# The experts' weight loads move from SyncE's DMA queue to GpSimd's

## The chip, the cores and the metric

The kernel runs on one core of one Trainium2 chip. The core has TensorE (PE, the matmuls), VectorE (DVE), ScalarE (ACT), GpSimd (POOL) and SyncE (SP), and 16 DMA engines that move data between HBM and the on-chip memory SBUF. A transfer is issued by one engine's instruction stream, in the order of the program, and goes into a queue that belongs to the issuer: in this kernel SP's transfers are in the queue that the profile calls q1 hardware_dynamic, and GpSimd's are in q0 software_dynamic. The metric is the device time of one execution in microseconds (us), lower is better.

## The reference, cut to what matters

One layer over 1024 tokens of width 1024. A mixer (a state-space scan and a gated short convolution, projected in and out) comes first; it is unchanged here. Then a mixture of 32 experts follows: the router picks two experts for each token, every expert computes `(silu(x @ w_gate) * (x @ w_up)) @ w_down` on its tokens with a hidden width of 512, and the two results of a token are added with their gates. A root-mean-square norm ends the layer.

```python
h  = x + mixer(rmsnorm(x))
hn = rmsnorm(h)
ys = lax.map(run_block, (xs, block_expert))          # (silu(xb @ w_gate[e]) * (xb @ w_up[e])) @ w_down[e]
out = zeros.at[row_token].add(ys * row_gate[:, None])
return rmsnorm(h + out)
```

All weights are float32. One expert has three matrices of 2 MB, so that the 32 experts bring in 201 MB, each byte used once.

## The kernel before, in words

The program is one long, hand-ordered instruction stream. Its first part, up to about 800 us, is the mixer in two halves of 512 tokens. Its second part walks over the experts. Each expert has a place for up to 96 tokens (`CAP`); what doesn't fit is done by a loop at the end, which runs no iteration on these data.

**Weights.** Each of the 96 matrices (32 experts, gate, up and down) comes in two halves of 1 MB, [128 partitions x 2048 floats], which makes 192 halves numbered q. `order` (line 785) is the order of the matrices: gate and up of the next expert stand before down of the present one. A half lands in one of 15 places (`HALVES`, line 792), which are regions of SBUF that the mixer left free: SC, P1, Y, P2 and WR hold two each, TA four, N one. `load_m` (line 816) issues the load of half q, by SP. The first 15 loads (q 0 to 14) are put into the stream by hand, at the end of the mixer. From then on `reuse` (line 800) issues one load each time a half has been used up: the place becomes the home of the next half. `reuse` also retires places: N is never reused, and a place of TA, WR, P2 or P1 is given up when the loads are more than `lead` halves ahead. `lead` falls from 15 to 8, and is 4 from the 150th half on (`Q1`, `LEAD1`), where only the four places in SC and Y are left.

**Splits and matmuls.** A half is used as two chunks of [128 x 1024], 384 chunks c in all. `split_m(c)` writes each chunk as two float32r parts into one of four W buffers: the high part by ACT (line 80), the rest by DVE (line 86). After the second chunk of a half it calls `reuse`. In loop step c (line 1222) PE multiplies chunk c, then whatever `between` holds for this place is put into the stream, then chunk c + 4 is split. Each chunk feeds six matmuls of 512 columns (lines 1123 to 1125 for gate and up, 1134 to 1136 for down).

**Gathers and scatters.** These are the indirect transfers, and GpSimd issues them. `gather(e)` (line 1093) fetches the rows of expert e's tokens from `hg_d` into one of two buffers GX; it is issued two experts ahead, after `tok_trans(e - 2)` (line 1109) has read the buffer. `down_out(e)` scales the result by ACT (line 1156) into one of four buffers YE and adds it to the rows of `acc_d` by an indirect transfer with addition (line 1157). Each scatter waits for the scatter before it, since both add to `acc_d`. Slots without a token carry an index out of bounds and move nothing.

**The end.** `fin_load` (line 1191) waits for the last scatter of the loop, of expert 30, and then loads the sums by SP, 8 tiles of 512 KB (line 1195). `fin_norm` (line 1199) normalises and stores them, and `fin_last` adds expert 31's result.

Which part is ordered by what: SP's and GpSimd's instructions run in program order, each after its waits. The loads wait for DVE's split of the half that lay in the place before. In the program, the loads from q 15 on stand between the gathers and scatters: the load of q 15 stands before the first gather, and the loads from q 16 on after it.

Of the kernel before, what the change touches and what calls it, by code (L numbers as in the profile page):

```python
# [35 lines left out]
def layer(ctx: ExitStack, tc: tile.TileContext, x, norm_mix, w_in, ssd_conv_w, ssd_conv_b, dt_bias,  # L36
# [16 lines left out]
    def region(tag, shape, dt=F32):  # L53
        return rg.tile(shape, dt, name=tag, tag=tag)
# [22 lines left out]
    act, dve, pe, pool, sp = nc.scalar, nc.vector, nc.tensor, nc.gpsimd, nc.sync  # L77
# [716 lines left out]
    NR = len(HALVES)  # L794
# [5 lines left out]
    def reuse(q):  # L800


        n = len(place)
        lead = max(LEAD, NR - q // FALL) if q < Q1 else LEAD1
        if HALVES[place[q]][0] == "N" or n - q > lead and HALVES[place[q]][0] in TAGS:
            return
        place[n] = place[q]
        load_m(n)

    def raw_half(q):  # L810
        tag, i = HALVES[place[q]]
        if tag not in raw:
            raw[tag] = region(tag, [P, {"TA": 8192, "N": 2048}.get(tag, 4096)])
        return raw[tag][:, i * 2048:(i + 1) * 2048]

    def load_m(q):
        if q < 2 * len(order):
            kind, e = order[q // 2]
            src = {"g": w_gate, "u": w_up, "d": w_down}[kind]
            sp.dma_start(raw_half(q), src[e, q % 2])  # L820

    def split_hi(c):
        copy_a(W[(NB + c) % 4][:, 0], raw_half(c // 2)[:, c % 2 * 1024:(c % 2 + 1) * 1024])
# [12 lines left out]
    for h in range(2):  # L836
# [25 lines left out]
        if h == 1:  # L862
            for q, n in enumerate((44, 44, 45, 46, 51, 47, 49, 55, 56, 57, 57, 58, 58)):
                at(b0 + n, load_m, q)
# [95 lines left out]
    h_stats(1, KD - 2)  # L960
    h_stats(1, KD - 1)
    load_m(13)
    load_m(14)
    reuse(0)
# [257 lines left out]
    for c in range(end):  # L1222
        kind, e = order[c // 4]
# [61 lines left out]
```

## Time and profile before

| | |
|---|---|
| median of 3 runs | 1439.19 us (1437.18 to 1439.37) |
| the profiled execution, its own time | 1442.68 us |
| its span, first to last instruction | 1440.8 us |
| mean granted TensorE clock | 0.98 |
| busy: PE, weight loads of PE, DVE, ACT, POOL | 95%, 72%, 71%, 62%, 9% |
| q1 hardware_dynamic (SP) | 291.06 MB, 56.0% of 16 engines' span |
| q0 software_dynamic (GpSimd) | 30.44 MB, 8.5% |

A busy share is the time in which an engine executes instructions, over the span; DMA shares are means over the 16 DMA engines. A row such as "POOL L1157 <- ACT N" says that an instruction of line 1157 on POOL had to wait, and that the last thing it waited for was an ACT instruction that writes N. The profiled execution is 3.5 us over the median.

### The profile page before, as it was taken

The page shows a single profiled execution, that of the slowest core. Times are in us where ns is not written, and L with a number is a line of the kernel's source. Part 1 is how long each engine was busy: PE and PEld are TensorE (multiplying, and loading weights), DVE is VectorE, ACT ScalarE, POOL GpSimd, SP SyncE. Part 2 cuts the span into 40 slices and gives each one's busy share as a digit, 9 for nine tenths or more (in the row PEclk, how much of TensorE's full clock was granted, in tenths as well). Part 3 has the DMA queues.
Part 4 walks back from the last instruction along what each step waited for, and adds up shares of the span by engine and source line. Part 5 has one row for each costly group of instructions (what it writes and reads, how often), then busy time and mean ns, then how long its engine had stood idle before and what let it go on. Part 6 is the DMA issues. An engine that isn't in the chain of part 4 may idle for free. (4 is left out here: it accounts for less than half of the span.)

```text
span 1440.8 us, 17497 instructions
## 1 busy us (share of the span) xinstructions
PE 1362.1 (95%) x6459; PEld 1044.3 (72%) x6459; DVE 1029.4 (71%) x1356; ACT 890.9 (62%) x1343; POOL 132.2 (9%) x123
## 2 busy tenths in 40 slices
PE   6999999999999999999999499999999999999992
PEld 4888888878878878888788376677777777776661
DVE  5755676664467776765643589999989998988884
ACT  5655434365365544433643487788888888887783
POOL 0000100200000000000000101111111111112110
PEclk9999999999999999999999699999999999999995
DMA  6333332543444233225565779899999999999996
GB/s 192 133 99 106 116 93 88 135 165 118 125 145 133 95 111 117 73 88 147 212 212 183 257 287 347 308 367 352 361 363 368 363 360 371 375 352 318 348 331 242
DMA packets 128453, 322.64 MB, mean 224 GB/s; under 512 B 8960, under 2 KB 89012, under 8 KB 103789
## 3 DMA queue, kind: packets, MB, share of 16 engines
q1 hardware_dynamic: 117164, 291.06, 56.0%
q0 software_dynamic: 11200, 30.44, 8.5%
q8 instruction: 51, 0.84, 0.2%
q14 instruction: 38, 0.30, 0.1%
HBM read 304.71 MB, written 25.30 MB: 229 GB/s over the span
## 5 line engine op out<-in xcount | busy, mean ns | idle before, releaser
L86 DVE TENSOR_TENSOR W<-WR,W 128x1024 fp32r<-128x1024 f32 (+1 forms) x162 | 195.1, 1209 | 108.7 <-ACT W L80 108.5
L1124 PE MATMUL acc<-W,TB 128*96 128x512 f32 x512 | 202.6, 396 | 5.6 <-DVE W L86 5.6
L1123 PE MATMUL acc<-W,TB 128*96 128x512 f32 x512 | 204.5, 399 | 0.7 <-ACT W L80 0.7
L1125 PE MATMUL acc<-W,TB 128*96 128x512 f32 x512 | 203.1, 397 | 0.0
L80 ACT ACTIVATE W<-WR 128x1024 fp32r<-128x1024 f32 (+1 forms) x162 | 168.3, 1043 | 34.2 <-PE acc L274 18.3
L257 PE MATMUL acc<-TA,W 128*128 128x512 f32 x416 | 165.7, 398 | 1.9 <-ACT tk L529 1.9
L257 PE MATMUL acc<-TB,W 128*128 128x512 f32 x416 | 166.0, 399 | 1.2 <-ACT tk L529 1.2
L259 PE MATMUL acc<-TB,W 128*128 128x512 f32 x416 | 162.3, 390 | 0.0
L259 PE MATMUL acc<-TA,W 128*128 128x512 f32 x416 | 162.3, 390 | 0.0
L258 PE MATMUL acc<-TA,W 128*128 128x512 f32 x416 | 162.0, 389 | 0.0
L258 PE MATMUL acc<-TB,W 128*128 128x512 f32 x416 | 162.0, 389 | 0.0
L86 DVE TENSOR_TENSOR W<-SC,W 128x1024 fp32r<-128x1024 f32 x96 | 114.4, 1218 | 20.0 <-ACT W L80 19.0
L86 DVE TENSOR_TENSOR W<-Y,W 128x1024 fp32r<-128x1024 f32 x92 | 109.4, 1218 | 15.0 <-ACT W L80 14.9
L1124 PEld LDWEIGHTS acc<-W,TB 128*96 128x96 f32 x512 | 83.1, 162 | 42.6 <-DVE W L86 9.0
L1125 PEld LDWEIGHTS acc<-W,TB 128*96 128x96 f32 x512 | 82.8, 162 | 35.8 <-DVE TB L86 0.4
L1123 PEld LDWEIGHTS acc<-W,TB 128*96 128x96 f32 x512 | 83.0, 162 | 35.1 <-ACT W L80 1.6
L80 ACT ACTIVATE W<-SC 128x1024 fp32r<-128x1024 f32 x96 | 98.6, 1057 | 13.1 <-DMA SC<-in_w_up_dram 6.8
L1135 PE MATMUL sd<-W,TB 128*96 128x512 f32 x256 | 102.4, 400 | 3.8 <-DVE W L86 3.8
L86 DVE TENSOR_TENSOR W<-P,W 128x1024 fp32r<-128x1024 f32 x80 | 95.4, 1218 | 13.5 <-ACT W L80 13.2
L1134 PE MATMUL sd<-W,TB 128*96 128x512 f32 x256 | 104.1, 407 | 1.0 <-ACT TB L80 0.6
L80 ACT ACTIVATE W<-Y 128x1024 fp32r<-128x1024 f32 x92 | 94.9, 1058 | 15.3 <-DMA Y<-in_w_up_dram 5.9
L1136 PE MATMUL sd<-W,TB 128*96 128x512 f32 x256 | 102.1, 399 | 0.0
(306 smaller groups left out, 2444.2 us busy)
## 6 DMA issues: line engine op xcount, KB each, us to landing
WR<-in_w_in_dram SPq DMA_DIRECT2D x44, 1024.0 KB, 5.1
SC<-in_w_down_dram SPq DMA_DIRECT2D x18, 1024.0 KB, 11.0
WR<-in_w_out_dram SPq DMA_DIRECT2D x16, 1024.0 KB, 6.3
SC<-in_w_gate_dram SPq DMA_DIRECT2D x16, 1024.0 KB, 12.1
P<-in_w_up_dram SPq DMA_DIRECT2D x16, 1024.0 KB, 9.1
Y<-in_w_up_dram SPq DMA_DIRECT2D x16, 1024.0 KB, 13.1
Y<-in_w_gate_dram SPq DMA_DIRECT2D x15, 1024.0 KB, 14.2
TA<-in_w_down_dram SPq DMA_DIRECT2D x15, 1024.0 KB, 9.9
```

Of the source, the lines that this page charges most:

```text
L80: act.activation(o, i, AF.Copy, scale=scale)
L86: dve.tensor_tensor(o, a, b, op=op)
L257: pe.matmul(o, w[:, 0, k], t[:, 0, k], start=start and k == 0, stop=False)
L258: pe.matmul(o, w[:, 0, k], t[:, 1, k], start=False, stop=False)
L259: pe.matmul(o, w[:, 1, k], t[:, 0, k], start=False, stop=stop and k == KD - 1)
L1123: pe.matmul(pt, a[:, 0, k], w[:, 0, q], start=k == 0, stop=False)
L1124: pe.matmul(pt, a[:, 0, k], w[:, 1, q], start=False, stop=False)
L1125: pe.matmul(pt, a[:, 1, k], w[:, 0, q], start=False, stop=k == KD - 1)
L1134: pe.matmul(pt, a[:, 0, k], w[:, 0, n], start=k == 0, stop=False)
L1135: pe.matmul(pt, a[:, 0, k], w[:, 1, n], start=False, stop=False)
L1136: pe.matmul(pt, a[:, 1, k], w[:, 0, n], start=False, stop=k == 3)
```

## The change

`load_m` issues the halves q 0 to 15 by SP as before (`NR` is 15), and the halves from 16 on, 176 of the 192, by GpSimd. Nothing else is edited: each load stands at the same place of the program and has the same source, destination and size. It is now in GpSimd's instruction stream, between the gathers and scatters, and in their DMA queue.

```diff
         if q < 2 * len(order):
             kind, e = order[q // 2]
             src = {"g": w_gate, "u": w_up, "d": w_down}[kind]
-            sp.dma_start(raw_half(q), src[e, q % 2])
+
+            (sp if q <= NR else pool).dma_start(raw_half(q), src[e, q % 2])
```

## Rows read from the trace of the kernel before

**Rows 1.** Busy time of each engine in stretches of the experts' part: stretch, its length, busy us (and instructions) of PE, PE's weight loads, DVE, ACT and POOL, granted clock, DMA share, GB/s.

```profile
934.00:952.00 18.00, 18.00 (x87) 12.77 (x86) 16.29 (x17) 15.21 (x19) 3.24 (x2) 1.00 0.99 358
...
1262.00:1280.00 18.00, 18.00 (x88) 12.77 (x87) 16.30 (x17) 15.39 (x19) 3.59 (x3) 1.00 1.02 374
...
1317.00:1337.00 20.00, 18.75 (x87) 12.53 (x87) 16.03 (x16) 15.04 (x19) 3.92 (x3) 1.00 1.00 359
1337.00:1357.00 20.00, 18.09 (x84) 12.10 (x82) 16.08 (x16) 14.37 (x19) 3.52 (x2) 1.00 0.98 347
```

**Rows 2.** GpSimd's instructions in order of time, here scatters (line 1157): start, us, line, what; in brackets the idle time before and what ended it. The first two are 18 experts apart, the last two 4.

```profile
943.44 1.43 POOL L1157 DMA_INDIRECT acc_d<-S,idx  x1 [9.68 <-ACT S L1156]
...
1261.20 1.43 POOL L1157 DMA_INDIRECT acc_d<-N,idx  x1 [9.68 <-ACT N L1156]
1278.85 1.43 POOL L1157 DMA_INDIRECT acc_d<-N,idx  x1 [9.68 <-ACT N L1156]
...
1357.21 1.43 POOL L1157 DMA_INDIRECT acc_d<-N,idx  x1 [12.45 <-ACT N L1156]
```

**Rows 3.** The weight loads of line 820 in two stretches, 1200 to 1285 and 1285 to 1400 us: who waited for them (us, times), and their time from issue to landing.

```profile
  ACT W L80: 2.3, 2
...
DMA to landing us min/median/max: 14.8/17.7/20.3
...
  ACT W L80: 17.8, 15
...
DMA to landing us min/median/max: 6.2/7.6/9.4
```

**Rows 4.** SP's DMA queue over the whole span: what its loads of line 820 waited for, us in total, times, longest.

```profile
SPq L820 <- DVE W L86: 499.4, 176, 16.0
```

**Rows 5.** SP's instructions in order of time: single loads around 1102 us, the first and the last of those with four places left (15 rows, 30 loads), and the loads of the sums at the end.

```profile
1102.18 0.33 SPq L820 DMA_DIRECT2D SC<-in_w_gate_dram  x1
...
1300.68 3.25 SPq L820 DMA_DIRECT2D SC<-in_w_up_dram  x2
...
1383.16 3.76 SPq L820 DMA_DIRECT2D Y<-in_w_up_dram  x2
1389.80 3.23 SPq L820 DMA_DIRECT2D SC<-in_w_down_dram  x2
...
1402.99 5.87 SPq L1195 DMA_DIRECT2D TA<-acc_d  x8
```

**Rows 6.** GpSimd's plain transfers of the mixer that fill 128 partitions too, with 4 KB a partition: duration in ns, min/median/max, first and last start.

```profile
L451 POOL DMA_DIRECT2D P<-acT_d x16: 527/528/597, 57.3 to 593.2; - x16
```

**Rows 7.** GpSimd's gathers and a scatter in order of time, columns as in rows 2: one gather at 831 us, a scatter and a gather of the steady part, and ahead of the scatter ScalarE's scaling that it waits for.

```profile
831.18 0.95 POOL L1093 DMA_INDIRECT TB<-hg_d,idx  x1 [4.78 <-PE acc L1109]
...
1100.80 1.25 ACT L1156 ACTIVATE g<-sd,tab 96x512 f32<-96x512 f32 x2
...
1102.32 1.43 POOL L1157 DMA_INDIRECT acc_d<-g,idx  x1 [9.68 <-ACT g L1156]
1108.49 1.81 POOL L1093 DMA_INDIRECT TB<-hg_d,idx  x1 [4.74 <-PE acc L1109]
```

**Rows 8.** VectorE in order of time around these two, and the duration in ns (min/median/max) of its splits of one region from 940 to 1260 us.

```profile
1100.93 1.23 DVE L86 TENSOR_TENSOR W<-SC,W 128x1024 fp32r<-128x1024 f32 x1 [0.62 <-ACT W L80]
...
1108.23 1.21 DVE L86 TENSOR_TENSOR W<-TA,W 128x1024 fp32r<-128x1024 f32 x1
...
L86 DVE TENSOR_TENSOR W<-TA,W x51: 1209/1218/1229, 939.1 to 1239.2; 128x1024 fp32r<-128x1024 f32 x51
```

**Rows 9.** Issues of 512 KB over the span by issuer: count, KB each, median us from issue to landing; both stand beside the mixer's loads.

```profile
P<-acT_d POOLq DMA_DIRECT2D x16, 512.0 KB, 4.1
...
WR<-in_w_in_dram SPq DMA_DIRECT2D x2, 512.0 KB, 3.8
```

**Rows 10.** The two DMA queues from 1100 to 1200 us (packets, MB, share of 16 engines), and the issues there of gathers and of scatters (count, median us to landing).

```profile
q1 hardware_dynamic: 4599, 33.50, 87.1%
q0 software_dynamic: 1232, 2.99, 12.9%
...
TB<-hg_d,idx POOLq DMA_INDIRECT x6, 9.5
acc_d<-N,idx POOLq DMA_INDIRECT x3, 8.9
```

**Rows 11.** The same from 57 to 62 us, where GpSimd's queue is alone: three transfers of 4 KB rows.

```profile
q0 software_dynamic: 298, 1.11, 63.6%
```

**Rows 12.** The same from 1102 to 1111 us.

```profile
q1 hardware_dynamic: 450, 3.28, 88.5%
```

**Rows 13.** The end in order of time: GpSimd's last two scatters, and ScalarE's scaling of expert 30's result, its first split of the last half, and the first norm.

```profile
1384.64 1.41 POOL L1157 DMA_INDIRECT acc_d<-g,idx  x1 [8.80 <-ACT g L1156]
1393.96 2.28 POOL L1157 DMA_INDIRECT acc_d<-N,idx  x1 [7.91 <-ACT W L80]
...
1389.23 1.24 ACT L1156 ACTIVATE N<-sd,tab 96x512 f32<-96x512 f32 x2
...
1399.77 1.06 ACT L80 ACTIVATE W<-SC 128x1024 fp32r<-128x1024 f32 x1 [0.71 <-DMA SC<-in_w_down_dram]
...
1408.49 1.06 ACT L1201 ACTIVATE junk<-TA 128x1024 bf16<-128x1024 f32 x1 [2.15 <-DMA TA<-acc_d]
```

**Rows 14.** TensorE in order of time: a matmul of the last matrix's third chunk, which the first split of the last half feeds.

```profile
1407.03 0.63 PE L1135 MATMUL sd<-W,TB 128*96 128x512 f32 x1
```

## The prediction

> **What bounds the kernel now.** I read the busy times of stretches first, then the waits, then the DMA queues, then the instructions in order of time. From 934 to about 1285 us TensorE is busy in every microsecond (18.00 of 18.00), and the DMA engines are busy too, share 0.99 to 1.02 [rows 1]. An expert takes (1261.20 - 943.44) / 18 = 17.65 us there [rows 2]. TensorE sets that pace, but transfers fall behind: the last loads before 1285 land a median 17.7 us after their issue, at most 20.3 [rows 3]. They may be eight halves ahead, and a half is used every 17.65 / 6 = 2.94 us, which gives 23.5 us; less about 4 us for the two splits that free a place, nothing is left over. So the lead is just used up when the code, from the 150th half on, goes down to four places. After that loads do end last: ACT waits 15 times for one, 17.8 us in all [rows 3], TensorE is busy 18.09 of 20.00 us at a DMA share of 0.98 [rows 1], and four experts take 78.36 us, 7.8 more than 4 x 17.65 [rows 2]. SP is no limit: it waits 499.4 us for DVE to free places [rows 4]. Hence the change can matter by the time from a free place to data in it, by what the engines move in a microsecond, and at the end, where norms wait for the last scatter.
>
> **The change part by part.**
>
> *Issuing.* SP loses 176 issues of 0.33 us [rows 5], 58 us in which nobody waited for it: 0. GpSimd gains 176 plain issues of a kind that it has issued only in the mixer. The nearest rows, also over 128 partitions, take 0.53 us [rows 6]; from above stands the scatter with 1.43 [rows 7]. I take the first, which has the same number of pieces: 93 us in all. With a gather of 1.81 and the scatter, six loads make 3.24 + 6 x 0.53 = 6.4 us of the 17.65, at the upper end 11.8, and there is room. The order also fits: at 1102.18 SP issues a load that DVE's split frees, and GpSimd's scatter follows at 1102.32 [rows 5, 7]; it would stand 0.4 us behind that load. The release of the next load is DVE's, behind ACT's split, which stands behind the scaling that releases the scatter; so in the steady part no load waits for an indirect transfer in front of it. 0.
>
> *Time from a free place to data.* SP starts 0.02 us after DVE's end (1100.93 + 1.23 = 1102.16, then 1102.18) [rows 5, 8]; GpSimd starts 0.27 us after ACT's release (1100.80 + 1.25 = 1102.05, then 1102.32) [rows 7] and needs 0.53 instead of 0.33. That makes 0.45 us more. Landing rows of 512 KB say 4.1 against 3.8 us, 0.3 [rows 9]. I take 0.45. Until 1285 it is hidden: the transfers stand in a queue of some six loads, so that a later issue shortens the waiting in it; without this cover it would cost 0.45 us an expert or more, about 9 us over 20 experts. Behind 1300 us four places turn round, 30 loads in 7.5 rounds [rows 5]: 7.5 x 0.45 = 3.4 us if only latency counts, 0 if the engines do, whose share is 0.98 to 1.00 [rows 1]. The share is nearer the second; I take +1.5.
>
> *One queue instead of two.* Bytes are the same. Today a gather lands after 9.5 us and a scatter after 8.9 [rows 10], both beside loads; tomorrow each waits for loads issued before it and holds up those behind it. Gathers are issued two experts, 35 us, ahead, and the scatter's buffer is needed again four experts later; 20 us don't hurt either. A scatter that has not landed in 17.65 us stops GpSimd before the next one, and the loads behind it with it, but the six loads then in the queue are 17 us of work: 0. What counts is whether the engines move loads as fast in this queue. In the saturated 100 us q1 needs 0.871 x 1600 us for 33.50 MB, 0.341 us for 8 KB [rows 10]. From above: GpSimd's queue alone needs 0.636 x 80 us for 1.11 MB, 0.188 us for 4 KB, 10% more per byte, starting and draining included [rows 11]. From below: in the quickest 9 us q1 needs 0.885 x 144 us for 3.28 MB, 0.318 us, 7% less [rows 12]. 10% more over 351 us and a tail of 90 us is +44 us; 7% less can only take what waiting there is, -8 us. The first row includes ramps and smaller pieces, the second is the loads themselves; I take no difference, 0.
>
> [...]
>
> *The end.* Expert 30's scaled result is ready at 1389.23 + 1.24 = 1390.5, yet its scatter starts at 1393.96, because the scatter of 1384.64 needs about 9 us [rows 10, 13]. Nine microseconds later SP issues the loads of the sums, at 1402.99 [rows 5], and ACT waits 2.15 us for the first [rows 13]. In one queue the first scatter stands behind loads issued up to 1383.16, which land by 1391 [rows 3, 5], and lands near 1393.5 as now. The second stands behind one issued at 1389.80, landing by 1397.4, and may land near 1400 instead of 1403; at most the 2.15 us can be gained. The last load now stands behind that scatter in GpSimd's stream: issued after 1396 instead of 1392.7, it reaches ACT about 3.5 us later than 1399.77, but its chunk is used only after 1407 [rows 13, 14]. From -2.1 to +3; I take -1.
>
> *Sum.* +1.5 - 1 = +0.5 on the profiled execution's 1442.68, so 1443.2. That execution is 3.5 us over the median shown; for the median it makes 1439.7, I say 1440. 0.2%, 2.9 us, is about what a measurement of this kernel can tell from no change.
>
> **The rivals.**
>
> *Faster: indirect transfers stop cutting in.* q0 takes 12.9% of the engines' time for 2.99 of 36.5 MB [rows 10], 1.7 times q1's price per byte. If part of that is the alternation between two queues, one queue gives up to 5% back, the lead isn't used up, and the 7.8 us of late loads go, with a part of the end. Against it: additions and scattered rows may be dear by themselves. 1439 - 7 = 1432.
>
> *Slower: the engines move loads more slowly out of GpSimd's queue.* For it speak the 10% of [rows 11]. It decides from about 1% on, since no lead is left at 1285: 3%, a third of that, is 10.5 us over the 351 us and 2.7 in the tail: 1439 + 13 = 1452.
>
> *Slower: GpSimd is held up by VectorE.* The gather takes 0.95 us where VectorE is free and 1.81 where a split of two SBUF inputs begins just before it (1108.23 to 1109.44) [rows 7, 8]. If plain issues suffer the same 0.86 us, each place is refilled 1.3 us later, 7.5 rounds x 1.3 = 10 us in the tail: 1449. Against it: sixteen plain issues in the mixer, beside VectorE's splits, all took 0.53 to 0.60 [rows 6]. VectorE itself is not slowed: its splits last 1209 to 1229 ns throughout [rows 8].
>
> [...]
>
> *It doesn't do what it says:* if the loads found their queue as before, the time is the same as in the forecast; this isn't a case of its own.
>
> **How the numbers follow.** Forecast 0.36 (1436.3 to 1442.1), faster rival 0.29, slower transfers 0.18, held-up issues 0.14, other losses (a late issue behind a scatter, the end) 0.03. So faster 0.29, same 0.36, slower 0.35. The likeliest case's own range is 1437 to 1442. As both signs hold much, the range takes in the faster rival and both slower ones: 1431 to 1455; beyond it lies the full 10% of [rows 11].
>
> **What would show it.** Right: experts 17.65 us apart until 1285; plain issues of 0.53 us on GpSimd; a saturated stretch at 360 to 375 GB/s; ACT's waits for loads near 18 us in the tail. Faster rival: above 375 GB/s, hardly any wait of ACT's. Slower: ACT waiting for loads before 1285 (transfers), or plain issues of 1.2 us and more (VectorE). I am wrong if loads wait behind gathers or scatters in GpSimd's stream in the steady part, or PE idles there.

## The result, and the profile after

The changed kernel takes 1461.38 us in the median of 4 runs (1460.09 to 1462.47), the kernel before in the same comparison 1439.28; the ratio is 1.0149 (95% interval 1.0134 to 1.0163). That is 22 us slower. I had said 1440, with a range that ended at 1455. The profiled execution took 1460.09 us, its span is 1458.3 us.

First the stretches, with the columns of [rows 1], one more of them at 1180:

```profile
934.00:952.00 18.00, 18.00 (x87) 12.84 (x86) 16.29 (x17) 15.39 (x20) 6.79 (x9) 1.00 1.00 361
1180.00:1198.00 18.00, 17.00 (x80) 11.53 (x79) 14.86 (x16) 11.96 (x15) 8.03 (x9) 1.00 0.93 326
1262.00:1280.00 18.00, 17.70 (x82) 11.66 (x80) 14.82 (x14) 13.35 (x18) 6.34 (x8) 1.00 0.96 348
1317.00:1337.00 20.00, 16.69 (x66) 9.59 (x65) 13.08 (x13) 13.63 (x17) 5.90 (x7) 1.00 0.95 307
1337.00:1357.00 20.00, 18.79 (x86) 12.30 (x85) 16.24 (x17) 15.08 (x20) 6.55 (x9) 1.00 1.00 339
```

TensorE is still busy throughout at 934 us. At 1180 it idles, at 326 GB/s; before, it was still fully busy at 1280 [rows 1]. The scatters, line 1158 now, show the pace (columns as in [rows 2]):

```profile
940.53 2.34 POOL L1158 DMA_INDIRECT acc_d<-S,idx  x1 [0.33 <-ACT W L80]
...
1102.76 4.19 POOL L1158 DMA_INDIRECT acc_d<-g,idx  x1 [1.62 <-ACT W L80]
...
1196.05 1.91 POOL L1158 DMA_INDIRECT acc_d<-N,idx  x1 [1.48 <-ACT W L80]
...
1295.35 1.63 POOL L1158 DMA_INDIRECT acc_d<-N,idx  x1 [1.39 <-ACT W L80]
```

The first is expert 4's, which was scattered at 943.44 before: the change starts 2.9 us ahead. Expert 13's is 0.4 us behind (1102.76 against 1102.32 in [rows 7]), the last one 16.5 behind (1278.85 in [rows 2]). The last five experts took (1295.35 - 1196.05) / 5 = 19.86 us each instead of 17.65. So the time was lost in the steady part, after 1100, where I had put nothing. Who waited is in the loads' own rows, 1200 to 1285 us, against [rows 3]:

```profile
  ACT W L80: 19.3, 9
...
DMA to landing us min/median/max: 18.6/19.2/19.6
```

ScalarE waited 19.3 us for loads, where it was 2.3. From 1285 to 1420 it waited 30.2 us, 18 times. And the data queues from 1100 to 1200 us (the share of 16 engines is the last number), against [rows 10]:

```profile
DMA packets 5633, 35.32 MB, mean 353 GB/s; under 512 B 962, under 2 KB 962, under 8 KB 1688
...
q0 software_dynamic: 5628, 35.25, 98.4%
```

The engines that move data were nearly as busy as before (98.4% against 87.1 + 12.9 = 100.0%) and moved 35.3 MB in the 100 us instead of the 36.5 (33.50 + 2.99) of [rows 10]: 3.2% less, about twice what the lower share explains. From 1000 to 1100 us the shares are all but equal, 85.8 + 13.7 = 99.5% before and 98.5 + 1.3 = 99.8% after, yet 3.7% fewer bytes move (before, then after):

```profile
DMA packets 5862, 36.23 MB, mean 362 GB/s; under 512 B 1043, under 2 KB 1043, under 8 KB 1845
...
DMA packets 5677, 34.88 MB, mean 349 GB/s; under 512 B 999, under 2 KB 999, under 8 KB 1849
```

The same bytes cost the engines more time. That leaves three theories: *Rate*, GpSimd's queue is slower as such; *Order*, loads are held up behind gathers and scatters in GpSimd's stream; *Gather* or *Scatter*, one of the two kinds of indirect transfer costs more in the loads' own queue.

### The profile page after: what moved, and what is told of

It is laid out like the page before. It is cut to its first block, busy times and chain, and to the rows that moved or that the text cites. A ratio compares the mean times of both kernels' runs of the same rounds, so it can differ in the third digit from the quotient of the medians.

```text
span 1458.3 us, 17495 instructions
## 1 busy us (share of the span) xinstructions
PE 1373.3 (94%) x6459; PEld 1039.7 (71%) x6459; DVE 1031.1 (71%) x1356; ACT 887.4 (61%) x1343; POOL 249.8 (17%) x299
## 5 line engine op out<-in xcount | busy, mean ns | idle before, releaser
L80 ACT ACTIVATE W<-SC 128x1024 fp32r<-128x1024 f32 x96 | 98.5, 1056 | 31.2 <-DMA SC<-in_w_up_dram 9.7
## 6 DMA issues: line engine op xcount, KB each, us to landing
Y<-in_w_gate_dram POOLq DMA_DIRECT2D x14, 1024.0 KB, 17.4
```

Source lines behind the costliest of these rows:

```text
L80: act.activation(o, i, AF.Copy, scale=scale)
```

## The experiments

**Without indirect transfers (e1, e2).** Gathers from expert 2 on and scatters are left out, with line 821 as before and as after.

```diff
-        if e < NE:
+        if e < 2:
             pool.indirect_dma_start(
                 out=GX[:, e % 2], out_offset=None, in_=hg_d,
...
-        pool.indirect_dma_start(
-            out=acc_d, out_offset=rows_of(R["idx"][:, e:e + 1]),
-            in_=y, in_offset=None, bounds_check=T - 1, oob_is_err=False, compute_op=OP.add)
```

> The loads by SP as before, and the loop's gathers (from expert 2 on) and scatters are left out, so that the routed results are not in the output. With nothing else in the engines than loads, the late loads of the tail should go in every theory: about 1430 us (1425 to 1436), TensorE at 17.65 us an expert to the end, engines at some 0.88 of their time.

> The same with the loads from half 16 on by GpSimd. Theory Rate (the engines move loads more slowly out of GpSimd's queue, whatever else is in it): 3.5% more engine time per byte than in the run by SP, but within the room that the missing gathers leave, so 1430 to 1436, at most 5 above the run by SP. Theory Order (loads are held up behind gathers and scatters in GpSimd's stream or queue): the same time as the run by SP within 2 us, and the same engine time per byte.

Measured: 1427.97 by SP (ratio to before 0.9912, 0.9895 to 0.9929), 1428.44 by GpSimd (0.9909, 0.9893 to 0.9926). With nothing else in the queue the change costs nothing. TensorE sets the pace here, though, so a slower queue could hide in the room.

**The light kernel, loads alone (e3, e4).** So that data transfers bound the experts' part, a third of the matmuls goes and the splits are halved:

```diff
-            split_hi(c)
-            split_lo(c)
+            split_one(c)
...
             pe.matmul(pt, a[:, 0, k], w[:, 0, q], start=k == 0, stop=False)
-            pe.matmul(pt, a[:, 0, k], w[:, 1, q], start=False, stop=False)
             pe.matmul(pt, a[:, 1, k], w[:, 0, q], start=False, stop=k == KD - 1)
```

> As the first run, and TensorE, VectorE and ScalarE lightened so that the engines that move data bound the experts' part: the product with the weights' low part (one third of the experts' matmuls) and the low parts themselves are left out, and every other chunk is split by VectorE instead of ScalarE. If TensorE's clock holds, an expert takes 15.3 to 16.4 us (768 rows of 8 KB at 0.318 to 0.341 us over 16 engines) instead of 17.65: some 1375 to 1410 us.

> The same with the loads from half 16 on by GpSimd. Theory Rate: 3.5% more of some 480 us, 14 to 20 us above the light run by SP. Theory Order: no more than 3 us above it, since nothing but loads is in the queue and in the stream.

Measured: 1314.32 (0.9114, 0.9099 to 0.9129) by SP and 1320.14 (0.9158, 0.9142 to 0.9173) by GpSimd. Both are far below my guess, since the engines move more than I had taken from [rows 10] and [rows 12]. The queues from 1000 to 1100 us, by SP:

```profile
DMA packets 5776, 42.10 MB, mean 421 GB/s; under 512 B 640, under 2 KB 640, under 8 KB 640
...
q1 hardware_dynamic: 5770, 42.03, 101.1%
```

and by GpSimd:

```profile
DMA packets 5915, 42.07 MB, mean 421 GB/s; under 512 B 655, under 2 KB 655, under 8 KB 911
...
q0 software_dynamic: 5622, 40.95, 98.5%
q1 hardware_dynamic: 288, 1.05, 2.6%
```

421 GB/s out of either queue: Rate is out. The 6 us between the two runs fit neither expectation. The 1.05 MB that SP moves in the second run are loads of the sums, which wait for no scatter there and come into the loads' time: 4.2 MB in all, some 10 us at 421 GB/s. So I don't put the 6 us down to the queue, though no run separates the two. From here on the last scatter stays in.

**Gathers alone, scatters alone (e5 to e8).** The same light kernel with the one or the other kind. For the scatters the first part of the first diff is kept; for the gathers its second part becomes

```diff
+        if e == NE - 2:
             pool.indirect_dma_start(
                 out=acc_d, out_offset=rows_of(R["idx"][:, e:e + 1]),
```

> The light kernel (third product, low parts and their matmuls left out) with its loads by SP and all gathers, but of the scatters only the last one; so the routed results are not in the output. The gathers bring 31 x some 64 rows of 4 KB, at 160 ns a row and engine some 0.7 us an expert: 1314 + 20 = 1334 us (1325 to 1345).

> The same with the loads from half 16 on by GpSimd. Theory Gather (the gathers, in the loads' own queue and stream, are what costs): 12 to 20 us above the run by SP. Theory Scatter (the additions are what costs): at most 5 us above it. Theory Rate has already lost: 420 GB/s out of either queue.

> The light kernel with its loads by SP and all scatters, but without the gathers from expert 2 on, so that stale rows are added. An added row takes 327 ns of an engine, twice a gathered one, 1.3 us an expert: 1314 + 40 = 1354 us (1335 to 1365).

> The same with the loads from half 16 on by GpSimd. Theory Scatter: 12 to 20 us above the run by SP. Theory Gather: at most 6 us above it.

Measured: gathers 1365.83 by SP (0.9492, 0.9473 to 0.9511) and 1405.45 by GpSimd (0.9779, 0.9750 to 0.9807), 40 us apart, where I had expected 12 to 20; scatters 1368.01 (0.9502, 0.9482 to 0.9521), 14 above my guess, and 1372.92 (0.9539, 0.9514 to 0.9564), 5 apart, no more than the loads alone. It is the gathers. By SP they cost more than I had expected, too: (1365.8 - 1314.3) / 30 = 1.7 us each, by GpSimd (1405.5 - 1320.1) / 30 = 2.8. GB/s in 40 slices of 2.5 us, 1000 to 1100 us, by SP:

```profile
GB/s 423 419 423 380 347 419 423 429 419 416 311 383 419 419 423 410 385 303 410 419 413 426 419 352 316 413 406 416 423 426 380 320 413 413 419 419 426 333 342 413
...
q0 software_dynamic: 672, 1.64, 5.3%
```

by GpSimd:

```profile
GB/s 403 328 316 321 383 334 369 359 362 310 351 383 403 377 387 369 316 380 377 308 315 375 305 360 377 375 377 359 356 356 324 375 364 400 321 315 411 297 362 364
DMA packets 5281, 35.56 MB, mean 356 GB/s; under 512 B 738, under 2 KB 738, under 8 KB 1150
...
q0 software_dynamic: 5275, 35.48, 100.9%
```

In its own queue a gather makes a dent of about two slices, down to some 310, about every 17 us (the gathers start at 1003.82, 1020.28, 1037.15, ...), and between them the loads run at 420. In the loads' queue no slice is above 411. By SP six gathers bring 1.64 MB in the 100 us, 4% of the bytes, and the rate falls from 421 to 397 GB/s. By GpSimd it falls to 356, by 15%, at a share of 100.9%: the engines are not idle, their rows are dearer.

Two ways in which a gather of 96 rows may differ from a load of 128, both theories, since no trace here names the engine of a row: (*Uneven*) some 64 of its 96 rows are real (the 1.64 MB of six gathers above are 67 rows of 4 KB each), and if an engine takes a run of 6 partitions, ten or eleven engines have 6 rows and the others none, fall out of step, and the rows behind them too; (*Ports*) if an engine's share of a gather isn't the share that it has of a load, the rows land among partitions that another engine is writing, which may slow the loads. If an indirect transfer over 128 partitions is dealt out to the engines as a load is, its rows stay clear of the other engines' loads; of the runs below that are this wide, the light ones agree with it (the width takes 53 to 55 us off).

**Rows dealt evenly, and by engine (e9 to e12).** Whole kernels again. In the first pair the partition of a token changes, nothing else:

```diff
+        pool.iota(jj[:, :CAP], pattern=[[1, 16], [16, 6]], base=0, channel_multiplier=0)
+        dve.tensor_copy(R["slotp"], jj[:, :CAP])
...
-            tt(o, R["slot"][:, None, :CAP].to_broadcast([P, NT, CAP]), pos.to_broadcast([P, NT, CAP]), OP.is_equal)
+            tt(o, R["slotp"][:, None].to_broadcast([P, NT, CAP]), pos.to_broadcast([P, NT, CAP]), OP.is_equal)
```

In the second pair the gathers and scatters of the loop are 128 partitions wide as well, and the dealing is another: each run of four partitions from 0 to 31 and from 64 to 95 gets four of the first 64 tokens. I call it "by engine" for its aim, four of these tokens for each engine; which engine has which partitions, no run shows. The widening:

```diff
-        R["idx"] = C([CAP, NE], "idx", I32)
+        R["idxp"] = C([P, NE], "idx", I32)
+        pool.iota(R["idxp"][CAP:], pattern=[[1, NE]], base=2 * T, channel_multiplier=0)
...
-    GX = EB[:CAP, 4608:6656].bitcast(F32).rearrange("p (s c) -> p s c", s=2)
+    GX = EB[:, 4608:6656].bitcast(F32).rearrange("p (s c) -> p s c", s=2)
...
-                in_offset=rows_of(R["idx"][:, e:e + 1]),
+                in_offset=rows_of(R["idxp"][:, e:e + 1]),
```

> The kernel before, whole, with the tokens of an expert dealt over the 96 partitions (rank r goes to partition 6 (r mod 16) + r div 16) instead of filling them from 0 on. Theory Uneven (each of the 16 engines takes a run of 6 partitions of an indirect transfer, so that with some 64 tokens ten or eleven engines move 6 rows and the others none, and the fullest engine sets when loads land): the fullest engine has 4 rows instead of 6 to gather and to add, 2 x (0.16 + 0.33) = 1 us less an expert, the late loads of the tail go: 1432 (1428 to 1436). Theory Ports (below): the rows still land beside the loads' rows: 1439.

> The kernel after with the same dealing out. Theory Uneven: the engines stay in step, so that the gather is through them in a few us: at least 12 us of the 22 come back, 1440 to 1449. Theory Ports: 1458 or more.

> The kernel before, whole, with the indirect transfers of the loop made 128 partitions wide like the loads (the last 32 indices out of bounds) and the tokens dealt so that each engine gets 4 of the first 64, if it takes the same partitions of an indirect transfer as of a load. Theory Ports (a gathered row slows the loads because it lands in partitions that another engine's load is writing): loads keep 312 ns a row beside gathers, 1 us less an expert, and the rows are even besides: 1428 to 1432. Theory Uneven alone: as the run with rows spread.

> The kernel after with the same. Theory Ports: the gathers in the loads' queue no longer slow it, nearly all of the 22 us come back: 1430 to 1443. Theory Uneven alone: as the run with rows spread. If the cause is neither, 1455 or more.

| loads by | as it was | rows spread | wide and by engine | wide only (below) |
|---|---|---|---|---|
| SP | 1439.28 | 1434.97, ratio 0.9955 (0.9939 to 0.9970) | 1434.05, 0.9957 (0.9943 to 0.9971) | 1442.22, 1.0011 (0.9998 to 1.0023) |
| GpSimd | 1461.38 | 1437.66, 0.9979 (0.9963 to 0.9994) | 1432.80, 0.9944 (0.9921 to 0.9966) | 1441.82, 1.0004 (0.9991 to 1.0018) |

All ratios are to the kernel before. The loads are where the change put them in the lower row, and with the rows dealt differently nothing of the 22 us is left; the one wide and by engine is 0.56% faster than the kernel before.

My ranges did not all hold. Spreading alone brought GpSimd's version to 1437.66, below the 1440 to 1449 of Uneven, so that spreading the rows is enough in the whole kernel. And by SP the wide transfers, dealt by engine, lie at 1434.05, not in the 1428 to 1432 of Ports but level with the rows spread, as Uneven alone would have it: there the width shows no gain.

The stretches of the kernel with rows by engine and loads by GpSimd, the same as above, its first and its twentieth scatter from expert 4 on, and the landing of its loads from 1200 to 1285 us:

```profile
1180.00:1198.00 18.00, 18.00 (x89) 12.88 (x88) 16.30 (x18) 15.04 (x18) 6.86 (x9) 1.00 1.00 388
1262.00:1280.00 18.00, 18.00 (x91) 12.91 (x90) 16.29 (x17) 15.04 (x18) 6.28 (x8) 1.00 1.00 393
1317.00:1337.00 20.00, 20.00 (x96) 14.21 (x95) 18.21 (x20) 17.09 (x21) 7.77 (x9) 1.00 1.00 373
...
940.02 2.49 POOL L1168 DMA_INDIRECT acc_d<-S,idx  x1 [0.31 <-ACT W L80]
...
981.98 5.90 POOL L1102 DMA_INDIRECT TB<-hg_d,idx  x1 [0.80 <-PE sd L1145]
...
1275.96 1.95 POOL L1168 DMA_INDIRECT acc_d<-N,idx  x1 [0.83 <-ACT W L80]
...
DMA to landing us min/median/max: 6.9/7.9/9.2
```

An expert takes (1275.96 - 940.02) / 19 = 17.68 us, TensorE is busy throughout, even at 1317, and loads land in 7.9 us instead of 19.2: the lead isn't used up. Loads, gathers and scatters stand in GpSimd's stream here exactly as in the changed kernel, so Order alone is out as the cause. The fifth line is a gather of 5.90 us that ends behind VectorE's splits, below; it cost nothing here.

**How much is Ports, how much Uneven (e13 to e16).** The light kernel with gathers alone shows it larger, with the edits of the two diffs above. The run "wide only" (e15) has the loads by GpSimd and the widening without a dealing.

> The light kernel with gathers alone and the loads by GpSimd (1405.5), rows dealt over the 96 partitions; third product, low parts and all scatters but the last left out. Theory Uneven, if it is all: the gathers cost only their rows, 64 x 0.16 / 16 = 0.64 us an expert, 1320 + 20 = 1340. Uneven and Ports together: the gather is over in a few us again, but loads beside it still take 450 ns a row: 1355 to 1375.

> The same, transfers 128 partitions wide and rows dealt by engine. Ports matter: loads at 312 ns a row throughout, 1335 to 1345, at least 12 us under the run with rows only spread. Ports don't matter: the same as that run.

> [...] Uneven alone: 1405 or more. Ports alone: 1335 to 1350. Both: in between, with the fullest engine at 8 x 0.16 = 1.3 us an expert, 1320 + 40 = 1360.

> The light kernel with gathers alone and the loads by SP (1365.8), wide and dealt by engine. Ports matter: 1335 to 1345, the same as by GpSimd. Ports don't matter, only the unevenness: about 1355.

Measured, where the kernel without these edits takes 1405.45: spread 1387.08 (0.9632, 0.9594 to 0.9670), wide and by engine 1334.19 (0.9263, 0.9248 to 0.9279), wide only 1350.50 (0.9374, 0.9358 to 0.9390); by SP, wide and by engine, 1331.84 (0.9246, 0.9223 to 0.9269). The two wide and by engine lie a little under my 1335 to 1345. The width gives 55 us and 53 (with the rows spread), the dealing 18 and 16: they add up, and the width is three times the larger. GB/s in slices of 2.5 us as above, rows spread over 96 partitions:

```profile
GB/s 293 308 339 416 426 403 282 259 300 383 423 423 426 336 300 356 421 419 418 287 270 290 344 393 423 423 349 297 279 357 387 429 419 397 323 279 351 385 419 403
```

wide and by engine:

```profile
GB/s 408 433 419 423 423 419 410 411 428 426 423 418 416 411 419 416 419 423 418 418 419 426 423 429 411 405 426 423 423 411 428 421 419 419 419 418 418 426 406 419
```

Spreading alone brings full-rate slices back between the gathers, but the dents stay, at 260 to 300; with the wide transfer and the dealing there are no dents at all. Wide only, dents to some 340 are left, and the mean is 403:

```profile
DMA packets 6202, 40.33 MB, mean 403 GB/s; under 512 B 1057, under 2 KB 1057, under 8 KB 1507
```

A gather wide and by engine costs (1334.2 - 1320.1) / 30 = 0.47 us by GpSimd and (1331.8 - 1314.3) / 30 = 0.58 by SP; the two times' intervals overlap. My guess for the spread rows (1355 to 1375) was 12 us too low, because I took the dent in the loads' queue to be as short as in a queue of its own; it is three to four slices here. For the width alone I had added 1.3 us an expert for a fullest engine with 8 rows (1360); no run shows the 8, and the kernel took 1350.50, at the edge of what I had given Ports alone.

**The width in the whole kernel (e17, e18).** The second diff alone, with the loads by GpSimd (e17) and by SP (e18).

> [...] Ports decide: 1433 to 1443. The unevenness decides here, since the additions count too: 1450 or more.

> [...] Ports decide: 1432 to 1438. The unevenness decides: 1440 or more.

Measured: 1441.82 and 1442.22, in the table. With loads by GpSimd the width alone takes back 20 us, where the dealing alone took back 24. With loads by SP it gains nothing: the time lies where I had put the theory Uneven (1440 or more). That range was worked out from a share of the rows for the fullest engine which no run shows. So in the whole kernel either edit is enough to take the loss back, and the width is shown to be the larger one only where transfers bound the kernel. Between the two queues no difference is left.

## Why the prediction was wrong, step by step

*What bounds the kernel* was right: TensorE sets the pace until the lead is gone, and what matters is what the engines move in a microsecond. Where the lead goes was not asked. It goes to the gathers and scatters, before the change as well: in the light kernel by SP a gather costs 1.7 us, of which (1365.8 - 1331.8) / 30 = 1.1 went with the wide, dealt rows, and a scatter (1368.0 - 1314.3) / 31 = 1.7.

*Issuing*: plain issues take 0.53 us, as taken, except for twelve of the 176, which show 0.85 to 1.14, ten of them just behind a scatter and two behind such a load. "No load waits for an indirect transfer in front of it" is wrong. GpSimd and VectorE of the changed kernel:

```profile
1034.09 0.53 POOL L821 DMA_DIRECT2D SC<-in_w_down_dram  x1 [2.35 <-DVE W L86]
1035.57 5.71 POOL L1094 DMA_INDIRECT TB<-hg_d,idx  x1 [0.95 <-PE sd L1137]
1041.29 0.59 POOL L821 DMA_DIRECT2D P<-in_w_down_dram  x1
1041.86 0.55 POOL L821 DMA_DIRECT2D Y<-in_w_gate_dram  x1
...
1035.78 1.21 DVE L86 TENSOR_TENSOR W<-P,W 128x1024 fp32r<-128x1024 f32 x1
1036.91 3.49 DVE L86 TENSOR_TENSOR W<-Y,W 128x1024 fp32r<-128x1024 f32 x3
1040.32 0.55 DVE L86 TENSOR_TENSOR TB<-sm,TB 128x384 fp32r<-128x384 f32 x1
1041.08 1.22 DVE L86 TENSOR_TENSOR W<-Y,W 128x1024 fp32r<-128x1024 f32 x1 [0.22 <-ACT W L80]
```

The gather ends just behind VectorE's row of four splits (1035.78 and 1036.91, to 1040.40), and two loads stand behind it. I had said that I would be wrong if loads wait behind gathers there, and they do; but that isn't where the time went. The kernel with rows by engine has a gather of 5.90 us, too, and 17.68 us an expert. The sign named for slow transfers, ScalarE waiting for loads before 1285, came true as well (19.3 us), and so did the idle TensorE.

*Time from a free place to data*: the price of 0.45 us can't be seen. With rows by engine GpSimd's version takes no longer than SP's (1432.80 and 1434.05, intervals overlapping), tail included.

*One queue instead of two* is the step that failed. The question was the right one, "whether the engines move loads as fast in this queue"; the answer "I take no difference, 0" was read from stretches in which gathers had a queue to themselves. A load alone is as fast in both queues (e3, e4: 421 GB/s). That a gather or scatter in one queue lands behind the loads issued before it held: by the landing signals, from 940 to 1285 us, 36 of the 39 before the change landed ahead of a load issued earlier, and none after it; the scatters that read N, from 1100 to 1200 us, land after 18.2 us instead of 8.9. With the gathers in it, the queue moved 3.2% less. I had noted that a gather "holds up those behind it" and gave it no price; it is 1.1 to 1.3 us each in the light kernel (2.8 against 1.7, or 40 us over 30 gathers), and once the lead is gone all of it is on the path. (A smaller slip: the 17.7 us beside the scatter's 8.9 is the median of a later stretch. From 1100 to 1200 us loads landed after a median 13.2, so a scatter still passed them.)

The whole kernel lost more, 19.86 - 17.65 = 2.2 us an expert, and its trace shows a limit that the prediction left out. SP's loads waited for DVE 176 times [rows 4] and once for a landing; from 1100 us on, GpSimd's wait for earlier loads to land:

```profile
SPq L820 <- DMA SC<-in_w_down_dram: 10.8, 1, 10.8
...
1112.55 0.57 POOL L821 DMA_DIRECT2D TA<-in_w_down_dram  x1 [0.65 <-DMA P<-in_w_down_dram]
1115.03 0.53 POOL L821 DMA_DIRECT2D TA<-in_w_down_dram  x1 [1.91 <-DMA P<-in_w_down_dram]
1117.57 0.53 POOL L821 DMA_DIRECT2D WR<-in_w_gate_dram  x1 [2.01 <-DMA SC<-in_w_gate_dram]
1122.09 2.51 POOL L1158 DMA_INDIRECT acc_d<-N,idx  x1 [3.99 <-DMA acc_d<-g,idx]
```

By the landing signals in the trace, 24 of the 26 loads from 1200 to 1285 us were issued 0.5 to 0.6 us after the transfer eight places before them in GpSimd's stream had landed. An expert is eight transfers there, six loads, a gather and a scatter; 19.2 us to land and 0.6 make 19.8, the pace that was measured. Before, SP's transfers had eight landing signals to themselves, and GpSimd's eight others (in the light kernel with gathers all 35 loads from 1000 to 1100 us follow the landing of the load eight before). In the kernel with rows by engine no load of that stretch waits in this way, as they land in 7.9 us, and the light kernel wide and by engine does wait so (31 of 38 loads from 1000 to 1100 us) and moves 419 GB/s. So the limit alone is not the cause, but it may make slow landings dearer; no run varied it. The last of these rows is a scatter that waits for the one before, with the loads behind it: the prediction had named that and put it at 0.

*The rivals.* "The engines move loads more slowly out of GpSimd's queue" had the sign and, with 3% for 3.2, the size of the loss in the stretch, but the wrong condition: it said from any queue of GpSimd's. With the tail its 3% made 13; the medians lie 22 apart, the profiled executions 1460.09 - 1442.68 = 17.4. "Held up by VectorE" named what happens to the gather, not to plain issues, and not the cause. "Indirect transfers stop cutting in" has it the wrong way round: in a queue of their own they cut in briefly (dents of two slices, e5), in the loads' queue they never leave (no slice above 411 GB/s, e6). A price of the alternation between two queues doesn't show: wide and by engine, a gather costs 0.58 us out of two and 0.47 out of one, the times' intervals overlapping.

*The end*, taken at -1, added nothing that shows: expert 30's scatter starts 17.9 us later than in [rows 13], and the span is 17.5 longer. The last load did come late. The scatter, SP's loads of the sums and ScalarE's wait for the last load:

```profile
1411.82 2.50 POOL L1158 DMA_INDIRECT acc_d<-N,idx  x1 [3.01 <-ACT W L80]
1413.79 1.12 POOL L821 DMA_DIRECT2D SC<-in_w_down_dram  x1
...
1418.03 4.84 SPq L1196 DMA_DIRECT2D TA<-acc_d  x8
...
1422.52 1.06 ACT L80 ACTIVATE W<-SC 128x1024 fp32r<-128x1024 f32 x1 [5.08 <-DMA SC<-in_w_down_dram]
```

The last load stands behind the scatter, and ScalarE waits 5.08 us for it; but the sums already come 15.0 us later than in [rows 5] (1418.03 against 1402.99).

## What to carry to other kernels

Before a transfer joins a queue, measure that queue with what will be in it: a stretch in which two kinds lie in two queues doesn't show what one queue does. A gather or scatter beside large loads should be as wide as they are (128 partitions, spare indices out of bounds) with its real rows dealt out as in the second pair: here the two together were worth 29 us with loads and gathers in one queue (1461.4 to 1432.8) and 5 in two (1439.3 to 1434.1), where the dealing alone gave as much and the width alone nothing. Look, too, at whether the transfers of the joined queue wait for each other's landing. When a share of 1.00 moves fewer bytes than another share of 1.00, look for what makes a row dearer.

## What the hardware showed that I had not expected

In the light kernel by SP a gather over 96 partitions pulls the engines' rate from 420 to about 310 GB/s while it runs; one over 128 with its rows dealt leaves no dent (411 to 426 GB/s in every slice, e16). Scatters, which read SBUF, showed no such gap between the queues (4.9 us, where the gathers had 39.6). That the cause is engines writing one another's partitions fits the light runs, but is argued: the rows of the trace don't say which engine moved them, and in the whole kernel with loads by SP the width gained nothing. Nor is it shown why a gather takes so much longer to pass in the loads' queue; that engines reach its rows at different times would explain it. The trace has sixteen landing signals for each load. If each is one engine's, the engines are out of step, before the change as well: from first to last signal the median load of 1200 to 1285 us takes 12.5 us before, 13.4 after and 2.2 with rows by engine; from 1000 to 1100 us in the light kernel with loads and gathers in one queue it takes 14.8 as it was, 8.1 spread, 11.9 wide only and 5.1 with both.

In these traces GpSimd's long gathers end just behind a split of VectorE's with two SBUF inputs. The gather at 1035.57 runs beside four that follow each other without a gap; the last ends at 1036.91 + 3.49 = 1040.40, and the gather 0.88 us later. VectorE's next instruction, which reads `sm` in PSUM, runs from 1040.32 to 1040.87 and leaves that distance as it is elsewhere. In the kernel before, a single split ends at 1109.44 [rows 8], and the gather beside it 0.86 us later, at 1110.30 [rows 7]. All gathers of the changed kernel that take over 1.1 us end 0.88 to 0.93 us after such a split, and so does the one of 5.90 us above (0.93). So a gather took 1.81 us beside one split and 5.71 beside four in a row; what holds it is not shown.
